# A decoder layer in four token blocks: the last block's side work ordered on four engines, one ring of four PSUM banks, the norm one tile sooner, attention's channels first in the out-projection

## The chip, the cores and the metric

The kernel runs on one core of a Trainium2 chip. The metric is the device time of one execution in microseconds (us). Several executions were timed, and one more was profiled; the rows of the profile and its trace are from that one. PE is TensorE (matrix products), DVE is VectorE, ACT is ScalarE, POOL is GpSimd, SP is SyncE, which here issues the DMAs. A time in a row counts from the start of the span.

## What is computed

One layer (DEPTH is 1) over 2048 tokens of width 1024, all in float32:

```python
h = rmsnorm(x, norm1)
q, k, v, b_gate, c_gate, hc, p = split(h @ w_in)       # 512, 128, 128, 256, 256, 256, 256 columns
attn_out = sliding_window_attention(q, k, v, sinks, rel_bias)   # window 128, 8 heads on 2 K/V heads
conv_out = short_conv_mixer(b_gate, c_gate, hc, conv_w)
pool_out = multiscale_pool_mixer(p, pool_w, pool_scale)
x = x + concatenate([attn_out, conv_out, pool_out]) @ w_out
h2 = rmsnorm(x, norm2)
x = x + square(relu(h2 @ w1)) @ w2
return rmsnorm(x, final_norm)
```

## The kernel before

A product of float32 matrices is made of three: each operand is split into a high part and a low part, and `mm3` (L273) adds high x high, high x low and low x high in one PSUM bank. So every weight tile is loaded by SP, its high part `wh` cast on ACT and its low part `wl` subtracted on POOL (some on DVE), five half tiles ahead of PE. The same split is made of everything that PE multiplies: `xh`/`xl` of the normed input, `pth`/`ptl` of the transposed probabilities, `mxh`/`mxl` of the mixed channels.

**Stage 1** runs over four blocks b of 512 tokens. A block has 14 projection tiles `pj{b}_{i}` of 24 products each, in the order of `IN_ORDER`: K, then queries, V, the pool and conv channels. From the fourth tile on, counted by n, attention runs between the tiles. It has eight units (j, g): 128 tokens j against K/V head g. A unit goes through scores `sc` (PE), `s`, `nm` (DVE), four exponentials (ACT), `rd` and a product (DVE), transposes `pt` (PE), casts `pth` (ACT) and `ptl` (DVE), products `av` with V (PE), copy and sum `ao` (ACT, DVE), and the split into `mxh` (ACT) and `mxl` (DVE or POOL). Each unit writes 128 columns of all four attention channels, rows 4 to 7 of `mxh`; rows 0 and 1 are the pool channels (through `ppm`, in `do_pmix`), rows 2 and 3 the conv channels (`bo`). Then `out_proj` (L715) makes eight tiles `po{b}_{c}` over the eight rows, 24 products each, adds x, stores x1, and sums its squares for the second norm.

PSUM has eight banks: `ps_mm` three for `pj` and `po`, `ps_sc` two for the scores, `ps_tr` two for transposes, norms and `ppm`, and `ps_av` one for `av`.

The next block's first norm is worked off between the out-projection's tiles c: squares at c = 0 and 1 (`norm_square`), the root at 2, its row stored at 3 and broadcast at 4, and the eight channels applied at 5 to 7 (`norm_apply`, rows `hf`, `xh`, `xl`).

In the last block, the second norm of the first 1024 tokens is prepared beside the rest: `first_blocks` (L795 on) loads four x1 tiles `xb` of 128x512 (step 0), scales them on DVE (step 1, four rows of L809) and combines them by four subtractions (step 2, L763), for four channel pairs k at the n that the table `FIRST` gives; the results are stored in `x2s`, whence the MLP reads its operands.

**The MLP** multiplies in two passes of 1024 tokens by a Strassen-like scheme with seven products (`B11`, `T2`, ... in `OPS`); its first products are `bB11`. The second norm of the last block is finished in its first steps, at the keys given to `on` (L1038 to L1040): root, row, broadcast. The second half (`o` tiles) goes over into the final norm: squares on ACT, summed on POOL into `acc3`, root (`final_rstd`), broadcast, scaling of `y` and stores.

The order on each engine is not that of the code: a scheduler places the instructions by priorities and its own idea of their durations, and keeps to buffers and data dependencies. `tc.issue_after(ins)` holds what is issued under it behind `ins`, on the engine of `ins` alone. Before, the last block's side work stood under

```python
with tc.issue_after(latest[0].ins):
```

where `latest[0]` is the last product on PE.

## Time and profile before

| | us |
|---|---|
| median of 3 runs (lowest, highest) | 1937.92 (1937.40, 1938.04) |
| the profiled execution's own time | 1936.93 |
| its span | 1935.2 |
| PE busy in it | 1892.6 |
| block 0's out-projection ends, block 1 begins | 175.9 |
| block 2 begins | 327.5 |
| block 3 begins | 479.1 |
| the MLP's first product | 648.3 |

The page gives busy times and shares of the span; the view of waits names for each engine what it waited for; the windows sum each engine's work between two times; a timeline or a chain of waits has one row for an instruction or a few alike, with its start, its length, its line and, in square brackets, how long the engine was idle before it and what ended that.

### The profile page before, as it was taken

Reading aid. Unit: us, or ns where it says so; the run is one execution under the profiler, and the core shown is the slowest. Engines: PE = TensorE matmul, PEld = TensorE weight load, DVE = VectorE, ACT = ScalarE, POOL = GpSimd, SP = SyncE. Lnnn points to the kernel's source line nnn. Section 1 sums busy time; section 2 is a strip of 40 time slices with the busy share of each in tenths; the row PEclk is TensorE's granted clock in tenths of the full one; section 3 lists DMA queues with packets and bytes.
Section 4 is the critical chain, followed back from the end, with each engine's and each line's share of the span. In section 5 each row is a group of like instructions: output and inputs, shape, how many; then the busy total and the mean of one; then the engine's idle time right before and its main releaser. Section 6 shows DMA issues by size and latency. Waiting matters only on the chain.

```text
span 1935.2 us, 25620 instructions
## 1 busy us (share of the span) xinstructions
PE 1892.6 (98%) x8507; PEld 1527.8 (79%) x8507; DVE 1123.6 (58%) x1423; ACT 895.9 (46%) x1640; POOL 1020.0 (53%) x748
## 2 busy tenths in 40 slices
PE   8999999999899999999999999999999999999997
PEld 5877887887687788888888888888888888888887
DVE  5785686585888577756574444442425264533465
ACT  5664674564367344554575545442323222225332
POOL 5666557565463655654464444434565665526521
PEclk9999999999899999999999999999999999999998
DMA  7327316425935779756685655578777566645344
GB/s 255 102 65 225 108 61 217 126 66 174 300 117 178 233 272 335 255 197 212 216 288 194 196 185 189 186 270 279 235 231 240 191 218 200 221 123 169 96 158 134
DMA packets 194136, 373.34 MB, mean 193 GB/s; under 512 B 22167, under 2 KB 30420, under 8 KB 194004
## 3 DMA queue, kind: packets, MB, share of 16 engines
q1 hardware_dynamic: 193768, 371.62, 59.6%
q8 instruction: 67, 1.10, 0.2%
q14 instruction: 65, 0.53, 0.1%
q10 hardware_dynamic: 236, 0.09, 0.0%
HBM read 248.41 MB, written 116.93 MB: 189 GB/s over the span
## 4 chain that ended last, share of the span: by engine, by line
PE 83%; DVE 7%; DMA 6%; issue 2%; ACT 1%; POOL 1%; SPq 1%; DVEq 0%; POOLq 0%; ACTq 0%
PE o L274 11%; PE o L275 11%; PE o L276 11%; PE bT L275 6%; PE bT L276 6%; PE bT L274 6%; PE bB L275 5%; PE bB L274 5%; PE bB L276 5%; PE pj L275 4%; PE pj L276 4%; PE pj L274 4%; DMA x1s<-xo 1%; PE pt L604 1%; DVE xl L406 1%
## 5 line engine op out<-in xcount | busy, mean ns | idle before, releaser
L253 POOL TENSOR_TENSOR wl<-wr,wh 128x512 fp32r<-128x512 f32 x354 | 499.2, 1417 | 502.4 <-ACT wh L252 462.1
L252 ACT CAST wh<-wr 128x512 fp32r<-128x512 f32 x416 | 254.3, 617 | 362.5 <-PE bT L275 66.9
L763 DVE TENSOR_TENSOR bl<-br,bh 128x1024 fp32r<-128x1024 f32 (+2 forms) x144 | 186.8, 1300 | 324.7 <-ACT bh L1111 323.8
L275 PE MATMUL o<-bl,wh 128*128 128x512 f32 (+1 forms) x960 | 363.4, 381 | 0.0
L276 PE MATMUL o<-bh,wl 128*128 128x512 f32 (+1 forms) x960 | 362.7, 381 | 0.0
L274 PE MATMUL o<-bh,wh 128*128 128x512 f32 (+1 forms) x960 | 351.1, 381 | 0.0
L275 PEld LDWEIGHTS o<-bl,wh 128*128 128x128 f32 x960 | 180.9, 188 | 38.3 <-DVE bl L763 0.2
L276 PEld LDWEIGHTS o<-bh,wl 128*128 128x128 f32 x960 | 180.8, 188 | 38.2
L274 PEld LDWEIGHTS o<-bh,wh 128*128 128x128 f32 x960 | 176.3, 188 | 38.0
L276 PE MATMUL bT<-hhT,wl 128*128 128x512 f32 x512 | 203.7, 398 | 0.0
L275 PE MATMUL bT<-hlT,wh 128*128 128x512 f32 x512 | 203.6, 398 | 0.0
L274 PE MATMUL bT<-hhT,wh 128*128 128x512 f32 x512 | 203.4, 398 | 0.0
L274 PE MATMUL pj<-xh,wh 128*128 128x512 f32 x440 | 176.7, 403 | 10.6 <-ACT wh L252 6.7
L275 PE MATMUL pj<-xl,wh 128*128 128x512 f32 x440 | 177.5, 403 | 6.1 <-DVE xl L406 5.8
L276 PE MATMUL pj<-xh,wl 128*128 128x512 f32 x440 | 176.2, 401 | 0.0
L253 POOL TENSOR_TENSOR wl<-s,wh 128x512 fp32r<-128x512 f32 x64 | 91.2, 1426 | 141.5 <-ACT wh L252 130.9
L252 ACT CAST wh<-s 128x512 fp32r<-128x512 f32 x64 | 39.7, 621 | 250.1 <-PE o L275 249.9
L275 PE MATMUL bB<-hlB,wh 128*128 128x512 f32 x384 | 152.3, 397 | 0.7 <-DVE hlB L967 0.7
L274 PE MATMUL bB<-hhB,wh 128*128 128x512 f32 x384 | 152.5, 397 | 0.0
L1111 ACT CAST bh<-br 128x1024 fp32r<-128x1024 f32 (+2 forms) x144 | 123.2, 857 | 63.3 <-PE o L276 57.6
L276 PE MATMUL bB<-hhB,wl 128*128 128x512 f32 x384 | 152.0, 396 | 0.0
L220 POOL TENSOR_TENSOR s<-wr,wr 128x512 f32<-128x512 f32 x64 | 128.5, 2008 | 14.9 <-DMA wr<-in_w_dram 10.2
(188 smaller groups left out, 3388.0 us busy)
## 6 DMA issues: line engine op xcount, KB each, us to landing
wr<-in_w_dram SPq DMA_DIRECT2D x256, 256.0 KB, 3.8
hop_T<-s SPq DMA_DIRECT2D x128, 256.0 KB, 3.1
wr<-in_win_dram SPq DMA_DIRECT2D x112, 256.0 KB, 4.4
hop_B<-h SPq DMA_DIRECT2D x96, 256.0 KB, 3.3
br<-hop_B SPq DMA_DIRECT2D x48, 512.0 KB, 4.4
br<-hop_T SPq DMA_DIRECT2D x48, 512.0 KB, 4.3
wr<-in_wout_dram SPq DMA_DIRECT2D x64, 256.0 KB, 2.9
wr<-ss_T SPq DMA_DIRECT2D x48, 256.0 KB, 2.8
```

What stands on the lines that cost most here:

```text
L220: gp.tensor_tensor(out=t, in0=a, in1=b, op=op)
L252: act.copy(hi, src)
L253: eng.tensor_tensor(out=lo, in0=src, in1=f32(hi), op=ALU.subtract)
L274: pe.matmul(ps, hi, xh, start=first, stop=False)
L275: pe.matmul(ps, hi, xl, start=False, stop=False)
L276: return pe.matmul(ps, lo, xh, start=False, stop=last)
L406: dve.tensor_tensor(out=xl[:, k], in0=hf, in1=f32(xh[:, k]), op=ALU.subtract)
L604: pe.transpose(ps[:, m * P : (m + 1) * P], s[:, m, kh * P : (kh + 1) * P], ident)
L763: return dve.tensor_tensor(out=out, in0=a, in1=b, op=ALU.subtract)
L1111: mark["act"] = act.copy(hi, src)
```

## The change

- `behind()` takes the place of `issue_after(latest[0].ins)`: it holds the last block's side work behind the latest instruction in the code on each of ACT, DVE, POOL and SP. `FIRST` moves some of its steps one n later.
- `ps_mm` has four banks, which `pj`, `av`, `ppm` and `po` share; `ps_av` is gone.
- `out_proj` multiplies rows 4 to 7 (attention) first, then 0 to 3, and its weights are loaded in that order.
- `do_pool(b, 1)` and `do_pmix(b, 1)` come one tile later.
- The next block's norm: all squares at c = 0, and every step one tile sooner, two channels applied at each of c = 4 to 7.
- The second norm of the last block takes its root, row and broadcast at (0, 1, 2), (0, 2, 4) and (0, 3, 2) in place of (0, 0, 2), (0, 1, 4) and (0, 3, 0).
- At the end, the last four squares are not added on POOL; PE sums them in PSUM by eight more products with a column of ones. The last stores go out from SP and ACT in turn.

```diff
-FIRST = ((0, 1, 2), (0, 3, 4), (3, 5, 6), (5, 7, 8))
+FIRST = ((0, 2, 3), (0, 3, 4), (4, 6, 7), (5, 7, 8))
...
+    sides = {e.engine for e in (act, dve, gp, sp)}
...
         for t in [win[c] for c in IN_ORDER] + [wout[c] for c in range(KC)]:
-            plan += [(plan_load(h), None) for h in halves(t)]
+            hs = halves(t)
+            plan += [(plan_load(h), None) for h in (hs if t.tensor is win.tensor else hs[::-1])]
...
+    @contextmanager
+    def behind():
+
+        with ExitStack() as order:
+            seen = set()
+            for ins in reversed(nc.cur_bb.bb.instructions):
+                if ins.engine in sides and ins.engine not in seen:
+                    seen.add(ins.engine)
+                    order.enter_context(tc.issue_after(ins))
+                    if len(seen) == len(sides):
+                        break
+            yield
...
-    ps_mm, s1 = opened("ps_mm", bufs=3, space=PSUM)
+    ps_mm, s1 = opened("ps_mm", bufs=4, space=PSUM)
...
-    ps_av, s4 = opened("ps_av", bufs=1, space=PSUM)
...
-    def rstd_of(acc, r, offs, psp, tag, name):
+    def rstd_of(accs, r, offs, psp, tag, name):
...
+        accs = accs if isinstance(accs, list) else [accs]
         for j, o in enumerate(offs):
-            pe.matmul(ps[:, j : j + 1], acc[:, o : o + P], ones, start=True, stop=True)
+            for i, acc in enumerate(accs):
+                pe.matmul(ps[:, j : j + 1], acc[:, o : o + P], ones, start=i == 0, stop=i == len(accs) - 1)
...
     def att_av(b, j, g, pts):
-        av = ps_av.tile([P, T], F32, tag="av", name=f"av{b}_{j}_{g}")
+        av = ps_mm.tile([P, T], F32, tag="mm", name=f"av{b}_{j}_{g}")
...
     def do_pmix(b, i):
         oh, ol = ct["p", i]
-        ps = ps_tr.tile([P, T], F32, tag="tr", name=f"ppm{b}_{i}")
+        ps = ps_mm.tile([P, T], F32, tag="mm", name=f"ppm{b}_{i}")
...
-        for k in range(KC):
-            if k % HC == 0:
+        for n in range(KC):
+            k = (n + HC) % KC
+            if n % HC == 0:
                 hi, lo = w_next()
...
-            mm3(ps, hi[:, k % HC], lo[:, k % HC], mxh[:, k], mxl[:, k], k == 0, k == KC - 1)
+            mm3(ps, hi[:, k % HC], lo[:, k % HC], mxh[:, k], mxl[:, k], n == 0, n == KC - 1)
...
             elif n == 7:
+                do_pmix(b, 0)
+            elif n == 8:
                 do_pool(b, 1)
-                do_pmix(b, 0)
-            elif n == 9:
+            elif n == 10:
                 do_pmix(b, 1)
...
-                with tc.issue_after(latest[0].ins):
+                with behind():
...
-                if c < 2:
-                    for k in range(2 + c * 6 // 2, 2 + (c + 1) * 6 // 2):
+                if c == 0:
+                    for k in range(2, KC):
                         norm_square(b + 1, k, dve)
+                elif c == 1:
+                    norm_rstd(b + 1)
                 elif c == 2:
-                    norm_rstd(b + 1)
+                    row_store(nr[b + 1], "n1", (b + 1) * T, T, ps_tr, "tr", f"n1_{b + 1}", tmp(f"row1_{b}"))
                 elif c == 3:
-                    row_store(nr[b + 1], "n1", (b + 1) * T, T, ps_tr, "tr", f"n1_{b + 1}", tmp(f"row1_{b}"))
-                elif c == 4:
                     norm_bcast(b + 1)
                 else:
-                    for k in {5: (0, 1), 6: (2, 3, 4), 7: (5, 6, 7)}[c]:
+                    for k in (2 * (c - 4), 2 * (c - 4) + 1):
                         norm_apply(b + 1, k)
...
-    on((0, 0, 2), norm2_rstd, NB - 1, psb, "b")
-    on((0, 1, 4), lambda: norm2_row(NB - 1, psb, "b", um("row2")))
-    on((0, 3, 0), norm2_bcast, 1)
+    on((0, 1, 2), norm2_rstd, NB - 1, psb, "b")
+    on((0, 2, 4), lambda: norm2_row(NB - 1, psb, "b", um("row2")))
+    on((0, 3, 2), norm2_bcast, 1)
...
-    def final_mul(p, n, f, cs):
+    def final_mul(p, n, f, cs, eng=sp):
...
-        late.append(lambda: sp.dma_start(outT[f * P : (f + 1) * P, a + cs.start : a + cs.stop], t))
+        late.append(lambda: eng.dma_start(outT[f * P : (f + 1) * P, a + cs.start : a + cs.stop], t))
...
+    w = TH // 2
+    acc3[1, 0] = [acc3[1, 0]]
     for j in range(HC):
-        final_square(1, 0, 2 * j + 1, cs, False)
+        if j % 2 == 0:
+            sq = pG.tile([P, TH], F32, tag="sq", name=f"sql_{j}", bufs=2)
+        t = sq[:, j % 2 * w : j % 2 * w + w]
+        act.activation(t, y_of(1, 2 * j + 1, 0, cs), AF.Square)
+        acc3[1, 0].append(t)
...
     for f in range(KC):
-        final_mul(1, 0, f, cs)
+        final_mul(1, 0, f, cs, act if f % 2 else sp)
         flush()
```

The order of instructions on the engines, at the three places that the prediction speaks of. (Lines in the changed kernel are 13 to 16 higher. The last number of a name is a running number.)

PE, block 1, the last two units of attention (`av1_2_1` and `av1_3_1`) and the first products of the out-projection. Before:

```order
L604 MATMUL pt1_2_1_1_2940<-ident_160,s1_2_1_2787 128x128 x4
L276 MATMUL pj1_7_3050<-xh1_1844,wl71_2908 128x512
L615 MATMUL av1_2_1_2961<-pth1_2_1_0_2936,VV_443 128x512
L616 MATMUL av1_2_1_2961<-ptl1_2_1_0_2937,VV_443 128x512
L604 MATMUL pt1_3_1_0_2998<-ident_160,s1_3_1_2880 128x128 x4
L274 MATMUL po1_0_3101<-mxh_446,wh72_2925 128x512
L275 MATMUL po1_0_3101<-mxl_447,wh72_2925 128x512
...
L615 MATMUL av1_3_1_3028<-pth1_3_1_1_3012,VV_443 128x512
L274 MATMUL po1_0_3101<-mxh_446,wh72_2925 128x512
L274 MATMUL po1_1_3152<-mxh_446,wh74_2992 128x512
L616 MATMUL av1_3_1_3028<-ptl1_3_1_1_3013,VV_443 128x512
```

And of the change, first at unit `av1_2_1`, ahead of tile `pj1_11`, then at the last unit, behind tile `pj1_7`:

```order
L617 MATMUL pt1_2_1_0_2921<-ident_160,s1_2_1_2784 128x128 x4
L629 MATMUL av1_1_1_2854<-ptl1_1_1_1_2839,VV_440 128x512
L617 MATMUL pt1_2_1_1_2930<-ident_160,s1_2_1_2784 128x128 x4
L628 MATMUL av1_2_1_2951<-pth1_2_1_0_2926,VV_440 128x512
L289 MATMUL pj1_11_2970<-xh1_1797,wh68_2723 128x512
...
L289 MATMUL ppm1_1_3082<-poh1_1_2966,pwh_435 128x512
L629 MATMUL av1_3_1_3025<-ptl1_3_1_0_3001,VV_440 128x512
L628 MATMUL av1_3_1_3025<-pth1_3_1_1_3009,VV_440 128x512
L629 MATMUL av1_3_1_3025<-ptl1_3_1_1_3010,VV_440 128x512
L290 MATMUL ppm1_1_3082<-pol1_1_2967,pwh_435 128x512
L291 MATMUL ppm1_1_3082<-poh1_1_2966,pwl_436 128x512
L289 MATMUL po1_0_3107<-mxh_443,wh72_2915 128x512
```

A unit's `av` was spread through a projection tile or between products of the out-projection. Now its first product stands ahead of the next tile, and the last unit's products stand directly ahead of the out-projection, whose first product (half tile `wh72`) reads the attention rows in place of the pool rows.

ACT, block 1, the copies and casts at the same place in the change (`ao` and `mxh` of the last unit, `sq2` the squares of the next block's norm, `mxh` of `ppm` and of `bo`):

```order
L636 COPY ao1_3_1_3036<-av1_3_1_3025 64x512
L389 ACTIVATE sq2_2_3088<-xr2_2_2306 128x512
L720 ACTIVATE mxh_443<-ppm1_1_3082,prm_159 128x512
L389 ACTIVATE sq2_3_3091<-xr2_3_2406 128x512
L667 CAST mxh_443<-bo1_1_3078 128x512
L641 CAST mxh_443<-ao1_3_1_3036 64x4x128
```

Before, the row of `ppm` stood ahead of this stretch; the other five are the same.

DVE, the out-projection of block 2, where block 3's norm is applied (`hf`, `xl`; `xo` ends an out-projection tile). Before:

```order
L406 TENSOR_TENSOR xl3_4867<-hf3_0_4868,xh3_4866 128x512
L406 TENSOR_TENSOR xl3_4867<-hf3_1_4872,xh3_4866 128x512
L809 SCALAR_TENSOR_TENSOR xb0_1_5263<-xb0_1_5263,prm_159,rb2_0_acc_5259 128x512
L724 TENSOR_TENSOR xo2_5_4876<-po2_5_4877,xo2_5_4876 128x512
L404 SCALAR_TENSOR_TENSOR hf3_2_4920<-xr3_2_3820,prm_159,rb3_4820 128x512
L404 SCALAR_TENSOR_TENSOR hf3_3_4924<-xr3_3_3920,prm_159,rb3_4820 128x512
L404 SCALAR_TENSOR_TENSOR hf3_4_4928<-xr3_4_4021,prm_159,rb3_4820 128x512
```

The change there, and further on in block 3 ahead of the last unit (`s3_3_1`):

```order
L422 TENSOR_TENSOR xl3_4820<-hf3_0_4821,xh3_4819 128x512
L422 TENSOR_TENSOR xl3_4820<-hf3_1_4825,xh3_4819 128x512
L738 TENSOR_TENSOR xo2_4_4829<-po2_4_4830,xo2_4_4829 128x512
L420 SCALAR_TENSOR_TENSOR hf3_2_4873<-xr3_2_3817,prm_159,rb3_4773 128x512
...
L607 TENSOR_TENSOR s3_2_1_5853<-s3_2_1_5853,rd3_2_1_5858 128x4x256
L823 SCALAR_TENSOR_TENSOR xb2_0_5657<-xb2_0_5657,prm_159,rb2_0_rb_5255 128x512
L823 SCALAR_TENSOR_TENSOR xb2_1_5658<-xb2_1_5658,prm_159,rb2_0_acc_5256 128x512
L823 SCALAR_TENSOR_TENSOR xb2_2_5659<-xb2_2_5659,prm_159,rb2_0_rb_5255 128x512
...
L606 RECIPROCAL rd3_3_1_5956<-den3_3_1_5955 128x4
```

The xb rows, of which three stood among the last rows of `hf` and `xl` and five more behind them, have left the out-projection of block 2: all 32 now stand inside block 3, eight of them ahead of the last unit's `rd`.

More of the change, by code (lines that the diff above doesn't have):

```diff
@@ L1 @@
 import math
-from contextlib import ExitStack
+from contextlib import ExitStack, contextmanager
 import numpy as np
@@ L275, in mm3 @@
         pe.matmul(ps, hi, xl, start=False, stop=False)
-        return pe.matmul(ps, lo, xh, start=False, stop=last)
+        pe.matmul(ps, lo, xh, start=False, stop=last)
     prm = cst.tile([P, NPAR], F32, name="prm")
@@ L482, in tile_trunk @@
     first = {}
-    latest = [None]
     def start_first(tiles):
@@ L510, in proj @@
                     mid()
-                latest[0] = mm3(ps, hi[:, k % HC], lo[:, k % HC], xh[:, k], xl[:, k], k == 0, k == KC - 1)
+                mm3(ps, hi[:, k % HC], lo[:, k % HC], xh[:, k], xl[:, k], k == 0, k == KC - 1)
         return ps
@@ L717, in out_proj @@
         ps = ps_mm.tile([P, T], F32, tag="mm", name=f"po{b}_{c}")
-        for k in range(KC):
-            if k % HC == 0:
+        for n in range(KC):
+            k = (n + HC) % KC
+            if n % HC == 0:
                 hi, lo = w_next()
-            if k == 0:
+            if n == 0:
                 sp.dma_start(xo, xT[c * P : (c + 1) * P, b * T : (b + 1) * T])
-            mm3(ps, hi[:, k % HC], lo[:, k % HC], mxh[:, k], mxl[:, k], k == 0, k == KC - 1)
+            mm3(ps, hi[:, k % HC], lo[:, k % HC], mxh[:, k], mxl[:, k], n == 0, n == KC - 1)
         dve.tensor_tensor(out=xo, in0=ps, in1=xo, op=ALU.add)
@@ L923, in tile_trunk @@
     flush()
-    for st in (sX, sB, s4, s3, s2, s1):
+    for st in (sX, sB, s3, s2, s1):
         st.close()
@@ L1142, in final_rstd @@
         r = cst.tile([P, 6], F32, tag="nr3", name=f"r3_{p}_{n}_{cs.start}", bufs=2)[:, : len(offs)]
-        rstd_of(acc3[p, n][:, cs], r, offs, psb, "b", f"n3_{p}_{n}_{cs.start}")
+        a = acc3[p, n]
+        rstd_of([a[0][:, cs]] + a[1:] if isinstance(a, list) else a[:, cs], r, offs, psb, "b", f"n3_{p}_{n}_{cs.start}")
         r3[p, n, cs.start] = r
```

## The prediction

> **What bounds the kernel now.** The page first (busy us, share of the span, instructions):
>
> ```profile
> PE 1892.6 (98%) x8507; PEld 1527.8 (79%) x8507; DVE 1123.6 (58%) x1423; ACT 895.9 (46%) x1640; POOL 1020.0 (53%) x748
> ```
>
> PE fills 98% of the span and no other engine comes near, so what counts is where PE stands still and where its clock is halved. The view of what PE waits for lists the standstills (us in total, times, longest), and the last row is the same view of 478 to 494 us alone:
>
> ```profile
> PE pj L275 <- DVE xl L406: 5.8, 7, 2.9
> PE sc L577 <- DMA q<-ql: 3.6, 5, 2.2
> PE pst_n L314 <- POOL acc L942: 3.5, 1, 3.5
> PE av L615 <- DVE ao L624: 3.2, 4, 1.9
> PE pj L274 <- ACT xh L405: 1.7, 1, 1.7
> PE pst_n L314 <- POOL acc L732: 1.2, 1, 1.2
> ...
> PE pj L275 <- DVE xl L406: 3.8, 3, 2.9
> ```
>
> Apart from the first load and the tail, these are nearly all the standstills there are. Next, sums over stretches of time: start:end and length, busy time of PE, PEld, DVE, ACT and POOL with instruction counts, granted clock of PE, DMA share, GB/s.
>
> ```profile
> 175.00:285.00 110.00, 108.42 (x535) 88.78 (x534) 76.45 (x106) 68.35 (x158) 68.54 (x63) 1.00 0.39 114
> 480.00:600.00 120.00, 108.61 (x506) 86.57 (x505) 104.04 (x134) 65.23 (x151) 65.64 (x51) 0.94 0.58 187
> 486.40:493.20 6.80, 3.89 (x9) 2.65 (x9) 6.80 (x7) 1.96 (x4) 3.85 (x3) 0.50 0.86 262
> 517.10:520.50 3.40, 3.12 (x9) 2.31 (x9) 2.21 (x4) 0.00 (x0) 0.00 (x0) 0.50 1.05 380
> 595.60:602.40 6.80, 6.35 (x19) 4.95 (x20) 5.87 (x10) 4.40 (x8) 1.28 (x1) 0.50 0.04 15
> 660.50:663.90 3.40, 3.40 (x9) 2.62 (x9) 1.21 (x2) 1.79 (x4) 0.00 (x0) 0.50 0.94 305
> ```
>
> Two things are seen. Block 1 (175 to 285) leaves DVE 33 us of slack; block 3 (480 to 600) has DVE busy for 104 of 120 us. And a standstill of PE costs twice: after the 2.9 us at 486, the 2.2 us at 516, the 1.9 us at 593 to 596 and the 1.2 us at 658, PE ran 3.4 or 6.8 us at half clock, half of which is lost.
>
> The Trainium skill ("TensorE: Matmul & The Clock Gate", section "What's actually happening") says that the array goes to half clock only after at least one idle window of about 3.4 us. The rows above disagree: standstills of 1.2 to 2.9 us were enough. By that rule of the Trainium skill my sum below would be 3.4 us less; it goes by the rows.
>
> **The change part by part.** *One ring of four banks, attention's channels first* (blocks 1 and 2). The rows of PE's order show two new things. First, `av` now takes a bank of the projections' ring, so its first product has to stand ahead of the next projection tile, directly behind the transposes that it needs: `av1_2_1` has 0.6 us of PE work (one `av` product and four transposes) between `pt1_2_1_0` and itself. In that time ACT must cast the transpose:
>
> ```profile
> 281.17 0.58 ACT L607 CAST pth<-pt 128x512 fp32r<-128x512 f32 x1
> 283.67 0.58 ACT L623 COPY ao<-av 64x512 f32<-64x512 f32 x1 [0.69 <-PE av L616]
> 284.28 1.16 ACT L373 ACTIVATE sq<-xr 128x512 f32<-128x512 f32 x2
> 285.33 0.60 ACT L654 CAST mxh<-bo 128x512 fp32r<-128x512 f32 x1
> 285.96 0.62 ACT L628 CAST mxh<-ao 64x512 fp32r<-64x512 f32 x1
> ```
>
> The cast is 0.58 us, behind up to one other ACT row of 0.6 us. So a unit waits for 0 to 0.8 us; walking the units of block 1 along ACT's order I get six waits of 0.15 to 0.8 us, **2.8 us** in all (bounds 0, if ACT always runs ahead, and 5).
>
> Second, the start of the out-projection. Each unit writes 128 columns of all four attention channels, so the first product of channel 4 needs the last unit. Before, channels 0 to 3 of three tiles stood there and covered it:
>
> ```profile
> 281.93 0.50 PE L615 MATMUL av<-pth,VV 128*128 128x512 f32 x1 [0.31 <-DVE ao L624]
> 283.19 0.40 PE L616 MATMUL av<-ptl,VV 128*128 128x512 f32 x1
> 288.34 0.40 PE L274 MATMUL po<-mxh,wh 128*128 128x512 f32 x1
> 289.04 0.40 PE L274 MATMUL po<-mxh,wh 128*128 128x512 f32 x1
> ```
>
> The last `av` product starts at 283.19 and the last `mxh` cast ends at 285.96 + 0.62 = 286.58: 3.4 us of chain (0.2 us of product, copy, two squares, cast of `bo`, cast of `ao`). Nobody saw it, since the attention half of the weights begins at 289.04 only. In the new order nothing but two `ppm` products (2 x 0.23 us) stands between the last `av` and the first `po`, and ACT's queue has the same rows plus the `ppm` cast (0.69 us, in place of one idle moment). PE waits 3.4 + 0.4 - 0.5, or **3.3 us** (bounds 2.0, if only copy 0.58, add 0.7, cast 0.62 and their hand-overs count, and 4.0). After a standstill of that length the rows above say one stretch of 3.4 us at half clock: **1.7 us** (bounds 0 and 3.4).
>
> What goes in these blocks: the 0.3 us of `av` on `ao` and the waits for `xl` at the block's start, since the next block's norm is worked off a tile sooner. Of their 5.8 us, 3.8 lie at the last seam, so 2.0 us in four waits are shared by two seams: 1.0 each. Per block 2.8 + 3.3 + 1.7 - 0.3 - 1.0 = +6.5, for two blocks **+13.0** (bounds +2 and +22).
>
> *Block 0.* DVE is what it waits for: busy 38.16 us of the 41 before its out-projection.
>
> ```profile
> 95.00:136.00 41.00, 37.63 (x168) 28.36 (x166) 38.16 (x52) 26.73 (x60) 24.63 (x23) 0.92 0.17 55
> ```
>
> The change takes nothing off DVE there; the waits move from inside the units to the start of the out-projection. I take **+1** (bounds -4, PE's own lost 41 - 37.6 us with the clock, and +5.5, the same stall and clock as block 1).
>
> *The last block's xb work ordered on four engines.* This gives the seam 2 to 3 back to `xl`: the 3.8 us at 479 to 490, the late `xh` of 1.7 us, and the half clock after it (6.8 / 2 = 3.4). In the same block go the 2.2 us wait for `q<-ql` with its clock (1.7), and by the fourth bank the 1.9 us with its clock (3.4). That would be 18 us. But the xb rows are not gone: in the new order all 32 stand between the third unit's scores and the last `mxl`. DVE's rows from 480 to 610 (busy, mean ns | idle):
>
> ```profile
> L763 DVE TENSOR_TENSOR xb<-xb,xb 128x512 f32<-128x512 f32 x16 | 13.1, 839 | 0.1
> L809 DVE SCALAR_TENSOR_TENSOR xb<-xb,prm,rb_rb 128x512 f32<-128x512 f32 x8 | 8.4, 1075 | 1.6 <-DMA xb<-x1s 1.6
> L406 DVE TENSOR_TENSOR xl<-hf,xh 128x512 fp32r<-128x512 f32 x6 | 8.1, 1403 | 0.0
> L809 DVE SCALAR_TENSOR_TENSOR xb<-xb,prm,rb_acc 128x512 f32<-128x512 f32 x7 | 7.4, 1051 | 2.2 <-DMA xb<-x1s 2.2
> L404 DVE SCALAR_TENSOR_TENSOR hf<-xr,prm,rb 128x512 f32<-128x512 f32 x3 | 3.1, 1076 | 0.0
> ```
>
> ```profile
> 479.08 0.40 PE L274 MATMUL pj<-xh,wh 128*128 128x512 f32 x1
> 599.69 0.78 PE L274 MATMUL po<-mxh,wh 128*128 128x512 f32 x1
> 648.33 0.40 PE L274 MATMUL bB<-hhB,wh 128*128 128x512 f32 x1
> 608.04 0.69 DVE L629 TENSOR_TENSOR mxl<-ao,mxh 64x512 fp32r<-64x512 f32 x1
> ```
>
> Block 3 starts at 479.08 and the MLP at 648.33: 169.25 us. The last `mxl` comes 129.0 us in, 8.4 us behind the first product of the out-projection, hidden again by channels 0 to 3. After the change the first scores stand behind four projection tiles (96 x 0.233 = 22.4 us, by the three products from 288.34 to 289.04) and some 4 us of small products and hand-over: DVE's part can begin 27 us in. It is 104.04 us less `xl` 8.1 and `hf` 3.1, which stand ahead of it, or 93; some early `ql` rows off and the last 9 us of the block on leave about 91. Of the 16 us in which DVE stood idle from 480 to 600, most fall to waits inside the units that the xb rows can now fill; walking the order I leave 4. So the last unit is ready 27 + 91 + 4 = 122 us in, its `mxh` at 121. Then come 192 products, 44.8 us, 1.7 us of half clock and 1 us of leftovers: 168.5 against 169.25. I take **0** (bounds -5, no idle DVE, and +7, 11 us of the 16 idle). The 18 us are given back as waits for DVE inside the units and at the out-projection, which has lost its cover.
>
> *The MLP's start.* The square sums of the last norm stand one row of products later, when POOL has long added: the 1.2 us, a following 0.3 and half of the 3.4 us at 660.5 go, **-3.2** (bounds -4, if the next wait goes with it, and -1.2).
>
> *The tail.*
>
> ```profile
> 1920.04 0.75 ACT L1136 ACTIVATE sq<-y 128x256 f32<-128x256 f32 x2 [3.67 <-DVE y L942]
> 1920.53 3.12 POOL L942 TENSOR_TENSOR acc<-sq,acc 128x256 f32<-128x256 f32 x4 [19.09 <-ACT sq L1136]
> 1928.78 3.77 SPq L1156 DMA_DIRECT2D out_dram<-y  x8
> 1929.14 2.35 DVE y L1152 x6
> ```
>
> POOL's four additions end at 1923.65. Without them four squares, two in 0.75 us, end 1.5 us behind 1920.04 or, with their waits for `y`, by 1921.8: 1.85 us sooner. The eight more products of 128x1 take some of it; no row has their price ahead of others, and at 0.08 us each, a third of the 0.23 of a full one, they cost 0.65: -1.2. SP issues a store each 3.77 / 8 = 0.47 us behind a DVE row each 2.35 / 6 = 0.39; two queues save the difference, 8 x 0.08 = -0.6. Together **-1.8** (bounds -3 and 0).
>
> Sum: 13.0 + 1 + 0 - 3.2 - 1.8 = **+9.0** on the profiled execution's own 1936.93 us, 1945.9. The median of the runs is 1937.92, 1.0 higher: 1946.9.
>
> **The rivals.** *PE sets block 3 after all.* If the xb rows run at their shortest (0.74 and 0.67 us against means of 1.06 and 0.84) DVE's part is 8 us shorter:
>
> ```profile
> L763 DVE TENSOR_TENSOR xb<-xb,xb x16: 670/679/1769, 499.1 to 540.6; 128x512 f32<-128x512 f32 x16
> L809 DVE SCALAR_TENSOR_TENSOR xb<-xb,prm,rb_rb x8: 734/752/1791, 492.7 to 524.7; 128x512 f32<-128x512 f32 x8
> ```
>
> PE's own work in block 3 is 169.25 less 18, or 151; with 2.8 + 3.3 + 1.7 that is 159, a gain of 10: sum -1, 1937. The long ones beside POOL speak against it.
>
> *The other side: ACT and DVE run a tile ahead.* With four banks PE takes up attention sooner; if ACT's casts are always there, no unit waits, and only the data's own chain of 2.0 us with 1.7 of clock is left: blocks 1 and 2 +2.4 each, block 3 at 151 + 3.7 = 154.7, -14.5, the rest -4: sum -13.7, 1924. It decides if the last `mxl` of block 3 comes before 110 us. For it: 33 us of DVE slack in block 1. Against it: the ACT rows between `av` and `mxh`, which stand there whatever DVE does.
>
> *DVE is later still in block 3*: each unit's wait holds up the next one's scores, since PE, ACT and DVE stand in each other's order; 10 us more, 1957.
>
> *The clock stays full after a standstill of 3.3 us*: 2 x 1.7 less, 1943.5. That is what the Trainium skill's rule would give. The four half-clock rows speak against it.
>
> That the xb work doesn't move is excluded by DVE's order, where the seam has none of its rows any more.
>
> **How the numbers follow.** Forecast 0.45, PE sets block 3 0.17, a tile ahead 0.20, later still 0.12, full clock 0.06. Some 0.2% (3.9 us) is what a measurement of this kernel tells from no change, so faster is under 1934.0 and slower over 1941.8. Faster: 0.20 and a little of the second case, 0.22. Same: 0.15 of the second and 0.05 of the forecast's low end, 0.20. Slower: the rest, 0.58. The range goes from 1927 (leaving out half of the tile-ahead case) to 1957 (half of the later case).
>
> **What would show it.** In the new profile: a wait of PE at each `po`, first row, on ACT's `mxh` of some 3 us in blocks 1 and 2, with a half-clock stretch behind it; small waits of `av` on `pth`; no wait for `xl` over 1 us at the last seam; block 3 near 169 us with DVE busy over nine tenths from 27 us on; no `pst_n` wait on L732; the tail's `pst_n` at about 1922. It is wrong if the out-projection starts without a wait, or if block 3 comes out under 160 us.

## The result, and the profile after

The changed kernel takes 1966.41 us in the median of 4 runs (1964.81 to 1967.01) against 1937.66 us (1935.4 to 1938.04, 4 runs) of the kernel before in the same sittings: ratio 1.015, 95% interval 1.0132 to 1.0167. It is slower, as forecast, but by 28.8 us where 9 were forecast, and above the range. Beside the runs of e1 to e4, one execution of the kernel before and one of e4 took over three times as long (6580 and 6490 us); they are left out of every figure.

The profiled execution took 1965.88 us, 28.95 more than that of before (1936.93). Cut at the first projection product of each block and at the MLP's first product, its trace gives (us):

| | block 0 | block 1 | block 2 | block 3 | MLP to the end |
|---|---|---|---|---|---|
| before | 175.9 | 151.6 | 151.6 | 169.2 | 1286.8 |
| after | 191.7 | 159.2 | 159.8 | 170.8 | 1282.7 |
| difference | +15.8 | +7.5 | +8.3 | +1.5 | -4.2 |
| forecast | +1 | +6.5 | +6.5 | 0 | -5.0 |

Four of the five terms came near, the last of them in part by luck, as the experiments show. Block 0 did not, and its 14.8 us too much are three quarters of the error.

The view of PE's waits, after (us in total, times, longest):

```profile
PE po L289 <- ACT mxh L641: 15.0, 4, 6.3
PE av L628 <- ACT pth L620: 9.9, 14, 2.1
PE sc L590 <- DMA q<-ql: 5.9, 2, 4.7
PE pt L617 <- DVE s L607: 2.5, 1, 2.5
PE sc L590 <- DVE s L594: 2.1, 2, 1.3
...
PE pj L290 <- DVE xl L415: 0.4, 2, 0.3
PE pst_n L330 <- ACT sql L1251: 0.3, 1, 0.3
```

The old waits are gone or small: `xl` from 5.8 to 0.4 us, and the waits of `pst_n` on POOL (1.2 and 3.5 us) are none, with 0.3 us on ACT in their place. Two new ones lead, the out-projection on the last unit's cast (four times, once a block) and `av` on the casts of the transposes. The third, scores waiting for a DMA, stands in block 0. The windows (start:end and length, busy PE, PEld, DVE, ACT, POOL, clock, DMA share, GB/s), first of before, then of after, show what the forecast had missed:

```profile
53.00:71.00 18.00, 17.46 (x87) 14.41 (x88) 12.13 (x16) 9.47 (x26) 12.19 (x13) 1.00 0.38 110
```

```profile
53.00:71.00 18.00, 9.14 (x36) 7.31 (x35) 11.50 (x19) 8.03 (x24) 2.43 (x4) 0.65 0.57 151
512.00:632.00 120.00, 109.03 (x511) 87.67 (x509) 93.78 (x130) 64.49 (x149) 61.24 (x47) 0.96 0.56 178
537.70:632.00 94.30, 83.33 (x392) 66.63 (x390) 85.99 (x110) 55.04 (x133) 48.15 (x37) 0.95 0.52 176
461.20:468.00 6.80, 6.50 (x15) 4.64 (x16) 4.55 (x6) 2.75 (x6) 1.33 (x1) 0.50 0.01 2
```

At block 0's first attention units PE made 36 products in 18 us instead of 87, at 0.65 of its clock. Block 3 (510.7 to 681.5) has DVE busy 93.8 of the 120 us from 512 on, 10 less than before; from 27 us into the block DVE is busy 86.0 of 94.3 us, the nine tenths that the prediction named as a sign. The last row is the half clock behind the out-projection's wait in block 2.

Block 1's out-projection on PE and ACT in the timeline of after (start, length, and in brackets idle time before and what ended it):

```profile
298.13 0.40 PE L628 MATMUL av<-pth,VV 128*128 128x512 f32 x1
298.37 0.39 PE L629 MATMUL av<-ptl,VV 128*128 128x512 f32 x1
298.60 0.39 PE L290 MATMUL ppm<-pol,pwh 128*128 128x512 f32 x1
298.83 0.39 PE L291 MATMUL ppm<-poh,pwl 128*128 128x512 f32 x1
302.32 0.97 PE L289 MATMUL po<-mxh,wh 128*128 128x512 f32 x3 [3.10 <-ACT mxh L641]
```

```profile
298.80 0.58 ACT L636 COPY ao<-av 64x512 f32<-64x512 f32 x1 [0.54 <-PE av L629]
299.40 0.63 ACT L389 ACTIVATE sq<-xr 128x512 f32<-128x512 f32 x1
299.94 0.67 ACT L720 ACTIVATE mxh<-ppm,prm 128x512 fp32r<-128x512 f32 x1
300.51 0.62 ACT L389 ACTIVATE sq<-xr 128x512 f32<-128x512 f32 x1
301.03 0.61 ACT L667 CAST mxh<-bo 128x512 fp32r<-128x512 f32 x1
301.66 0.61 ACT L641 CAST mxh<-ao 64x512 fp32r<-64x512 f32 x1
```

This is the chain that the prediction had read from the trace of before: on ACT a copy, two squares, the rows of `ppm` and `bo`, and the cast that PE waits for, back to back, and 3.10 us of wait where 3.3 were forecast.

### The profile page after: what moved, and what is told of

Read it like the earlier page. It is cut to its first block, busy times and chain, and to the rows that moved or that the text cites. A ratio compares the mean times of both kernels' runs of the same rounds, so it can differ in the third digit from the quotient of the medians.

```text
span 1964.1 us, 25655 instructions
## 1 busy us (share of the span) xinstructions
PE 1904.0 (97%) x8523; PEld 1537.2 (78%) x8523; DVE 1131.5 (58%) x1423; ACT 900.8 (46%) x1640; POOL 1025.1 (52%) x744
## 4 chain that ended last, share of the span: by engine, by line
PE 88%; DVE 5%; ACT 3%; DMA 2%; issue 1%; POOL 0%; SPq 0%; DVEq 0%; ACTq 0%; POOLq 0%
PE o L289 11%; PE o L290 11%; PE o L291 11%; PE bT L291 6%; PE bT L290 6%; PE bT L289 6%; PE bB L290 4%; PE bB L289 4%; PE bB L291 4%; PE pj L289 4%; PE pj L290 4%; PE pj L291 4%; PE po L290 3%; PE po L289 3%; PE po L291 3%
## 5 line engine op out<-in xcount | busy, mean ns | idle before, releaser
L255 POOL TENSOR_TENSOR wl<-wr,wh 128x512 fp32r<-128x512 f32 x354 | 506.8, 1436 | 574.5 <-ACT wh L254 526.0
L289 PE MATMUL bB<-hhB,wh 128*128 128x512 f32 x384 | 152.4, 397 | 0.0
```

What stands on the lines that cost most here:

```text
L255: eng.tensor_tensor(out=lo, in0=src, in1=f32(hi), op=ALU.subtract)
L289: pe.matmul(ps, hi, xh, start=first, stop=False)
```

## The experiments

Each run's blocks, from its own profiled execution (us; the last column is the run's difference to before in those executions' spans). e5 to e8, e11 to e13, e16 and e17 are single runs; of the others the profiled execution is one of several, and not always a middle one: that of e3 was the longest of five (1951.7 us, median 1947.5), that of e2 the shortest of four.

Pairs of runs with the same order of instructions say how far such numbers carry. Before, e10 and e14 have the same order on every engine up to the MLP, and differ by up to 4.7 us in block 0 and 1.9 in blocks 1 and 2. e5 and e17 have it in block 3, but for one row moved on each of PE, DVE and ACT, and differ by 6.5 us there. The change, e13 and e16 have the same order on PE in the whole MLP, and differ by up to 4.8 us there. Smaller differences of single executions say nothing by themselves.

| run | block 0 | 1 | 2 | 3 | MLP on | all |
|---|---|---|---|---|---|---|
| before | 175.9 | 151.6 | 151.6 | 169.2 | 1286.8 | |
| after | 191.7 | 159.2 | 159.8 | 170.8 | 1282.7 | +28.9 |
| e1, ring undone | 181.4 | 159.0 | 158.5 | 176.2 | 1285.4 | +25.3 |
| e2, attention first undone | 187.5 | 155.9 | 155.4 | 167.9 | 1282.8 | +14.2 |
| e3, both undone | 182.5 | 153.1 | 156.4 | 170.0 | 1288.0 | +14.7 |
| e4, xb order alone | 175.4 | 151.5 | 152.3 | 175.3 | 1286.8 | +6.1 |
| e5, av one tile later | 188.4 | 156.9 | 156.9 | 174.4 | 1283.8 | +25.1 |
| e6, ring alone | 186.3 | 155.0 | 155.8 | 181.5 | 1284.6 | +28.0 |
| e7, attention first alone | 181.7 | 159.3 | 158.2 | 172.8 | 1284.9 | +21.6 |
| e8, pool later alone | 181.5 | 153.1 | 154.8 | 167.9 | 1287.0 | +9.0 |
| e9, norm, norm2, tail | 174.6 | 154.5 | 150.4 | 168.1 | 1290.0 | +2.4 |
| e10, norm2, tail | 174.9 | 153.5 | 152.2 | 168.6 | 1288.3 | +2.4 |
| e11, all but the xb order | 191.7 | 158.4 | 159.2 | 173.0 | 1282.6 | +29.7 |
| e12, squares behind the last unit | 191.2 | 157.3 | 157.2 | 173.1 | 1286.6 | +30.1 |
| e13, block 0's av out of the ring | 192.6 | 159.5 | 158.4 | 172.9 | 1287.4 | +35.5 |
| e14, tail alone | 179.7 | 152.4 | 153.4 | 168.8 | 1284.5 | +3.5 |
| e15, norm, tail | 177.4 | 154.4 | 150.7 | 170.1 | 1287.6 | +5.0 |
| e16, pj0_2 behind the broadcast | 186.5 | 158.4 | 159.2 | 170.3 | 1285.7 | +24.9 |
| e17, e16 and e5 | 185.4 | 155.3 | 156.1 | 180.9 | 1283.1 | +25.7 |

### e1 to e4: parts undone, and the xb order alone

e1 takes the ring out of the change:

```diff
-    ps_mm, s1 = opened("ps_mm", bufs=4, space=PSUM)
+    ps_mm, s1 = opened("ps_mm", bufs=3, space=PSUM)
...
+    ps_av, s4 = opened("ps_av", bufs=1, space=PSUM)
...
-        av = ps_mm.tile([P, T], F32, tag="mm", name=f"av{b}_{j}_{g}")
+        av = ps_av.tile([P, T], F32, tag="av", name=f"av{b}_{j}_{g}")
...
-        ps = ps_mm.tile([P, T], F32, tag="mm", name=f"ppm{b}_{i}")
+        ps = ps_tr.tile([P, T], F32, tag="tr", name=f"ppm{b}_{i}")
```

> The change with the ring alone undone (three banks for the projections and the out-projection, one for av, the pool mix back in the transposes' banks). Theory R (the shared ring: a projection tile can't take its bank before av of the unit ahead has taken one, so PE stands at block 0's first scores with no tile to work on): block 0 ends 12 to 14 us sooner (near 178 us instead of 191.7), the waits of av on pth (9.9 us) fall under 2 us, the wait at the out-projection (3 us a block) stays; in all near 1948 us. Rival D (block 0 is late since DVE is, by the pool work issued one tile later and the earlier norm): block 0 ends within 3 us of 191.7, in all 1958 to 1963 us.

Measured: 1961.9 us, ratio to before 1.0115 (1.0099 to 1.0131). Block 0 is 10.3 us shorter, less than theory R's 12 to 14 but far from D's 3, so the ring does cost there; the waits of `av` on `pth` vanish from block 1. The total misses R's 1948 us: block 3 is 5.4 and the MLP 2.8 us longer, which no theory had, and blocks 1 and 2 gain nothing, since with a bank of its own the last unit's `av` waits for `ao` instead (block 1's waits):

```profile
PE po L289 <- ACT mxh L645: 2.6, 1, 2.6
PE av L632 <- DVE ao L641: 2.2, 1, 2.2
```

e2 puts the out-projection back in its old order (`for k in range(KC)`, the weights as before).

> The change with the order of the out-projection alone undone (pool and conv channels first, weights loaded in that order); the ring stays. Theory O (the out-projection has lost its cover): the waits of po on mxh (15.0 us in the change) fall under 2 us, blocks 1 and 2 take 153 to 155 us instead of 159.2 and 159.8; block 0's first scores still wait 8 to 9 us and half its 13 us loss or more stays, block 0 near 188 us; in all 1945 to 1950 us. Rival (the wait at the out-projection only moves): PE waits as long a few products later, for channels 4 to 7, and the time falls by under 4 us, 1962 to 1966.

Measured: 1953.75 us, ratio 1.0076 (1.0058 to 1.0094). In block 1 the wait of `po` is 0.2 us, not 3.1, and does not come again at channels 4 to 7:

```profile
PE av L630 <- ACT pth L622: 2.5, 4, 1.4
PE po L288 <- DVE ao L639: 0.2, 1, 0.2
```

Blocks 1 and 2 are 3.3 and 4.4 us shorter, block 0 4.2. The total missed its upper end by 4 us; in the part that theory O is about it stands.

e3 has both undone.

> The change without the ring and without attention's channels first: what is left is the xb work behind four engines, the pool work one tile later, the norm one tile sooner, the second norm's later keys and the tail. If the two parts taken out carry the whole loss: blocks 0 to 2 as before the change or 1 us shorter each, block 3 by 5 to 10 us shorter than 169 us, MLP and tail 4 us shorter: near 1924 us (1918 to 1930). Rival (block 3's DVE with all xb rows inside it is the bound, or the earlier norm takes DVE time from the last units): 1934 to 1942 us.

Measured: 1947.48 us, ratio 1.004 (1.0025 to 1.0055), slower than both cases expected: what is left of the change is no gain, and block 0 is still 6.6 us longer than before. e8 asks whether the later pool mix does that.

e4 puts the xb order alone into the kernel before (`behind()` and `FIRST`).

> The kernel before with only the xb work ordered behind the four engines and the FIRST table of the change. Theory S (the xb rows at the last seam cost PE what the seam lost): the 3.8 us wait for xl and the 1.7 us for xh at 479 to 490 and the half clock behind them (3.4) go, block 3 is 5 to 9 us shorter, in all 1929 to 1933 us. Rival (block 3 is bound by DVE, so the xb rows cost the same inside it): block 3 within 2 us of 169 us, 1936 to 1940 us.

Measured: 1945.92 us, ratio 1.0027 (1.0012 to 1.0043); slower, against both. The seam's `xl` waits do fall to 1.4 us, yet block 3 is 6.1 us longer. Its waits there:

```profile
PE av L630 <- DVE ptl L622: 3.5, 4, 1.5
PE po L288 <- DVE xo L738: 2.9, 1, 2.9
PE pt L618 <- DVE mxl L722: 2.8, 1, 2.8
PE pj L288 <- ACT ct L650: 2.3, 1, 2.3
PE pj L288 <- DVE bo L667: 1.7, 1, 1.7
```

Most wait for DVE rows, which here stand among xb rows: from 580 to 612 us DVE is busy 31.3 of 32 us. The xb work does not cost the same inside block 3 as at the seam, it costs more.

### e5 to e8: the ring's order, and each part alone

e5 issues each unit's `av` in the middle of the next tile, so that this tile takes its bank first:

```diff
+            av = []
             def mid(n=n):
+                if 3 <= n < 11:
+                    av.append(att_av(*st2.pop(n - 1)))
                 if 2 <= n < 10:
                     st2[n] = att_trans(*st1.pop(n - 2))
...
-            if 2 <= n < 10:
-                av = att_av(*st2.pop(n))
```

> The whole change, the ring of four kept, but each unit's av is issued in the middle of the next projection tile, so that this tile takes its bank first. Theory R (what counts in block 0 is that av stands ahead of the next tile in the ring): the tiles pj0_12 and pj0_13 stand ahead of av0_0_0 and av0_1_0, PE's waits between 53 and 71 us fall from 8.8 to under 4 us, block 0 takes 180 to 184 us instead of 191.7, and av no longer waits for pth (9.9 us to under 3). The wait of po on mxh stays at 3 us a block or grows; in all 1950 to 1957 us. Rival (the ring costs by its number of banks, whatever its order): block 0 188 us or more, in all over 1960 us.

Measured: one run, 1962.12 us. The waits from 53 to 71 us fall from 8.8 to 5.6 us, where theory R had under 4, and block 0 is only 3.3 us shorter, at 188.4 us: block and total are the rival's.

e6 has the ring alone, e7 attention's channels first alone, e8 the later second pool mix alone, each in the kernel before.

> The kernel before with the ring of four as the only edit. Theory R: block 0 takes 184 to 188 us against 175.9, blocks 1 and 2 are 2.5 to 4 us longer than 151.6 (waits of av on pth), in all 1950 to 1956 us. Rival (the ring alone is harmless, it needs the later pool work or the earlier norm beside it): block 0 under 179 us, in all under 1943 us.

> The kernel before with attention's channels first in the out-projection as the only edit. Theory O (lost cover, 3.3 us of chain and 1.7 of half clock a block): blocks 1 and 2 take 156 to 159 us against 151.6, block 3 3 to 8 us more than 169.2, block 0 2 to 6 us more than 175.9; in all 1952 to 1962 us. Rival (only the ring's order exposes the chain): blocks 1 and 2 under 153.5, in all under 1943 us.

> The kernel before with only do_pool(b, 1) and do_pmix(b, 1) one tile later. In the run without ring and attention's channels first, block 0 was 6.6 and block 1 1.4 us longer than before the change. Theory P (the second pool mix comes too late): block 0 180 to 183 us against 175.9, blocks 1 and 2 1 to 2 us more, in all 1943 to 1949 us. Rival N (the earlier norm takes DVE and ACT from the last units): within 2 us of the kernel before in every block.

Measured (one run each, 1965.02, 1958.58 and 1946.02 us). The ring alone costs 10.4 us in block 0 and 3.4 and 4.3 in blocks 1 and 2. Its total is 9 us over what was expected, all in block 3, where two waits lead:

```profile
PE bB L274 <- DVE xo L723: 6.8, 1, 6.8
PE sc L576 <- DVE s L580: 5.8, 2, 4.3
PE pj L275 <- DVE xl L405: 3.4, 2, 2.9
```

Attention first alone costs 7.6 and 6.7 us in blocks 1 and 2, 5.8 in block 0, and 3.5 in block 3; theory O is right on every block, within 0.3 us. The later pool mix alone costs 5.6 us in block 0, as theory P has it. The two hide each other there: with both and no ring (e1) block 0 is 181.4, no longer than with either alone.

### e9, e10, e14, e15: what is left as a gain

> The kernel before with three parts of the change: the norm one tile sooner, the second norm's later keys, and the tail. By the first prediction's terms for them: blocks 1 and 2 0.5 to 1 us shorter each (waits for xl), block 3 0 to 3 us shorter, MLP and tail 3 to 5 us shorter (1282 to 1284 us against 1286.8): 4 to 9 us faster than before in the same job. Rival (the earlier norm takes DVE and ACT time from the last units): block 0 2 us or more longer, in all within 3 us of before.

> The kernel before with the second norm's later keys and the tail only. Blocks as before (within 1 us), MLP and tail 3 to 5 us shorter: 3 to 5 us faster. Rival (the waits at the MLP's start move to the next operand that stands there): under 2 us.

> The kernel before with the tail only (the last four squares summed on PE, stores from two queues). From the last products' start to the end 12.8 us instead of 15.2, all blocks within 1 us of before: 2 to 2.5 us faster, ratio 0.9987 to 0.9990. Rival (the gain is lost at the stores' landing): under 1 us.

> The kernel before with the norm one tile sooner and the tail, without the second norm's later keys, which in the run with all three made the MLP 4 us longer (1277.1 us from its first product to the last tile's, against 1271.6). If those keys did that: MLP back at 1271 to 1273 us, block 0 near 174.7, blocks 1 and 2 together 303 to 305, in all 4 to 6 us faster than before, ratio 0.997 to 0.998. Rival (the earlier norm itself moves the MLP's first operands): MLP 1275 us or more, no faster than before.

Measured, 11 or 12 runs each: e9 1.0011 (1.0001 to 1.0022), e10 0.9996 (0.9983 to 1.0009), e14 0.9993 (0.9982 to 1.0004), e15 0.9991 (0.998 to 1.0001). e9 and e15 were expected 4 to 9 and 4 to 6 us faster than before, e10 3 to 5, e14 2 to 2.5; none shows it, though the interval of e14 still holds its number. The tail itself does what it should: in the traces of e9, e10 and e14 the end comes 12.83 us behind the last product's start, in that of e15 13.12, before 15.24. The other two parts do not show. In e10, with the new keys, no wait of `pst_n` on POOL is left at the MLP's start, but other operands are waited for (waits of 640 to 760 us):

```profile
PE bB L275 <- DVE hlB L969: 2.0, 2, 1.3
PE bT L274 <- ACT hhT L968: 1.0, 1, 1.0
PE bT L275 <- DVE hlT L969: 1.0, 2, 0.7
```

That the keys do it is not shown: e14, without them, waits 0.3 us for `pst_n` and the same 2.0 us for `hlB`, and e15, also without, 3.2 us for `pst_n`. From the MLP's first product to the last, before takes 1271.6 us, e14 1271.65, e10 1275.5, e9 1277.1, e15 without the keys 1274.5, and e6 and e7, which have none of these three parts, 1269.4 and 1269.6. No version of the parts is shown to beat the kernel before.

### e11 and e12: the xb order within the change, and ACT's queue

> The change with the xb work left as it was before (hoisted over the last seam). The ring alone took 181.5 us in block 3, the xb order alone 175.3, both with the rest 170.75. Theory C (the ring holds PE at the last seam's first scores, and the xb rows there make it longer, so with the ring the xb order is worth more than it costs): block 3 178 to 184 us, blocks 0 to 2 as in the change, in all 1970 to 1977 us. Rival (the xb order costs its 6 us here too): block 3 163 to 168 us, in all 1957 to 1961 us.

Measured: one run, 1966.69 us, as the whole change; block 3 takes 173.0 us. Both cases missed. The xb order, worth 6.1 us the wrong way alone, is worth 2.2 the right way here, within the spread. The 181.5 us of the ring alone in block 3 hold a wait of 6.8 us at the MLP's first product that this run doesn't have; e17 has one of 4.5 us there and e5, with nearly the same order, none.

e12 orders the next norm's squares behind the last unit's cast on ACT:

```diff
-        act.copy(hi, o)
+        last_mx[0] = act.copy(hi, o)
...
+                    with tc.issue_after(last_mx[0].ins):
+                        for k in range(2, KC):
+                            norm_square(b + 1, k, dve)
```

> The change, with the next norm's six squares ordered behind the last unit's mxh cast on ACT. If the 3.1 us wait at the out-projection of blocks 1 and 2 is a queue on ACT (two squares of 0.6 us between the copy and the cast), it falls to 2.0 to 2.5 us and the blocks are 0.6 to 1.5 us shorter. Rival (the chain through DVE or the half clock sets it, and ACT's squares lie beside it): 2.9 us or more, blocks within 0.4 us of 159.2 and 159.8.

Measured: one run. The wait in block 1 falls to 2.1 us, blocks 1 and 2 are 1.9 and 2.7 us shorter (the total is lost again in block 3 and at the MLP, by less than the spread of single runs there). Of the 3.1 us, 1.0 is ACT's queue and 2.1 the data's own chain.

```profile
PE po L289 <- ACT mxh L644: 2.1, 1, 2.1
```

### e13, e16, e17: why the ring costs in block 0

e13 takes `av` of block 0 alone out of the ring:

```diff
+        pool, tag = (ps_mm, "mm") if b else (ps_tr, "tr")
-        av = ps_mm.tile([P, T], F32, tag="mm", name=f"av{b}_{j}_{g}")
+        av = pool.tile([P, T], F32, tag=tag, name=f"av{b}_{j}_{g}")
```

> The change, with av of block 0 alone taking a bank of the transposes' pool in place of the projections' ring; all else, and all other blocks, as in the change. Theory R (block 0 is late because av0_0_0 stands ahead of pj0_12 in the ring, so that PE comes to the first scores with no tile left): the waits between 53 and 71 us fall from 8.8 to under 3 us, no half clock there, block 0 takes 179 to 184 us instead of 191.7; blocks 1 and 2 stay at 159 to 160; in all 1953 to 1959 us. Rival (block 0's end is set by DVE and the late pool mix, and the first stall only moves): block 0 188 us or more.

Measured: one run, 1972.5 us. The waits from 53 to 71 us are 1.3 us, without half clock, and block 0 is still 192.6 us. Theory R falls in its simple form: the stall that looked so large is gone and the block is as long as before the edit. Block 0's waits in this run:

```profile
PE pt L620 <- DVE ao L641: 3.3, 2, 1.7
PE sc L593 <- DVE s L597: 2.9, 1, 2.9
PE pt L620 <- DVE s L610: 2.7, 1, 2.7
PE po L289 <- ACT mxh L645: 2.4, 1, 2.4
```

The first of them is of the edit's own making (transposes waiting for the bank that `av` holds), the others are the units' own chain: scores, softmax, transposes.

What the kernels with four banks up to here have in common is another row, the first softmax row on DVE. Before, after, and in e13:

```profile
55.37 0.69 DVE L581 SCALAR_TENSOR_TENSOR s<-sc,bias 128x512 f32<-128x512 f32 x1 [2.05 <-PE sc L578]
```

```profile
62.38 0.69 DVE L594 SCALAR_TENSOR_TENSOR s<-sc,bias 128x512 f32<-128x512 f32 x1 [4.06 <-PE sc L591]
```

```profile
61.41 0.69 DVE L597 SCALAR_TENSOR_TENSOR s<-sc,bias 128x512 f32<-128x512 f32 x1 [0.23 <-PE sc L594]
```

It is the first of eight, one for each unit, and comes 7.0 us later than before. The lateness is not simply kept: the third unit's row comes at 69.7 us against 69.1 before, the fourth at 81.0 against 75.2, the eighth at 116.3 against 108.6. Whether the start sets the rest is what e16 tests. Why the chain starts later stands on PE, in the products that broadcast block 0's norm, without which no tile can be evacuated. Before, after:

```profile
39.33 0.83 PE L356 MATMUL pbc_n<-ident,r 128*128 128x128 f32 x6
```

```profile
36.20 0.39 PE L289 MATMUL pj<-xh,wh 128*128 128x512 f32 x1
...
45.21 1.05 PE L372 MATMUL pbc_n<-ident,r 128*128 128x128 f32 x8
```

The tile `pj0_2` is the fourth to ask for a bank of `ps_mm`. With three banks it had to wait for an evacuation, and so for the broadcast. With a fourth bank PE takes it at 36.20, its 24 products ahead of the broadcast, which comes 5.9 us later. e16 orders that tile behind the broadcast:

```diff
+                if b == 0 and n == 1:
+                    order.enter_context(tc.issue_after(pbc))
                 ps = proj(b, i, mid)
```

> The change, with the products of block 0's tile pj0_2 ordered behind the four products that broadcast the first norm. In all kernels with three banks for the projections the first softmax row s0_0_0 came at 55 to 56 us; in all with four, at 61 to 62, av's place in the ring or not: the fourth bank lets PE take pj0_2 (24 products, 5.6 us) ahead of that broadcast, on which every evacuation of the first tiles waits. Theory L (block 0 is set by the chain of its eight units, which starts 6 us late): s0_0_0 at 55 to 57 us, block 0 takes 183 to 187 us instead of 191.7, blocks 1 and 2 as in the change; in all 1957 to 1961 us. Rival (av's place in the ring sets it): s0_0_0 sooner, but block 0 still 189 us or more.

Measured: one run, 1961.87 us. The broadcast, the first softmax row, and block 0 at 186.5 us, as theory L has it:

```profile
39.97 1.05 PE L372 MATMUL pbc_n<-ident,r 128*128 128x128 f32 x8
```

```profile
56.83 0.69 DVE L597 SCALAR_TENSOR_TENSOR s<-sc,bias 128x512 f32<-128x512 f32 x1 [1.99 <-PE sc L594]
```

Against the change all eight softmax rows come 5.4 to 6.4 us sooner, and the block is 5.2 us shorter: in the order of the ring the start does carry through to the end. Against the kernel before, the rows from the fourth on are back within 1.7 us (the eighth at 109.9 us), and yet the block is 10.6 us longer. What is left of the loss comes behind the last unit's softmax. There the traces of e1, without the ring, and of e16 differ so, first e1, then e16:

```profile
132.11 0.69 DVE L641 TENSOR_TENSOR ao<-av,ao 64x512 f32<-64x512 f32 x1 [1.29 <-ACT ao L640]
132.84 0.61 ACT L645 CAST mxh<-ao 64x512 fp32r<-64x512 f32 x1 [0.76 <-DVE ao L641]
```

```profile
132.53 0.68 DVE L534 TENSOR_TENSOR z<-pj,rb 128x512 f32<-128x512 f32 x1
134.49 0.69 DVE L640 TENSOR_TENSOR ao<-av,ao 64x512 f32<-64x512 f32 x1
136.87 0.61 ACT L644 CAST mxh<-ao 64x512 fp32r<-64x512 f32 x1
```

The last product of the last projection tile starts at 117.0 us in e1 and at 129.8 in e16, between the last unit's `av` products. So in e16 the row that evacuates this tile (`z`) and one of the conv channels stand on DVE ahead of the last unit's sum `ao`, and the cast that the out-projection waits for comes 4.0 us later than in e1. No edit tests this reading.

e17 has e5's edit with it.

> The change with both edits to the order: pj0_2 behind the norm's broadcast, and each unit's av behind the next tile's start. Alone, the first took 5.2 us off block 0 and the second 3.3, of the 10.3 us that undoing the ring takes off. If the late start and av's place are two separate parts of the ring's cost: block 0 takes 181 to 184 us, near the 181.4 without the ring. Rival (the two edits mend the same thing): 186 us or more.

Measured: one run, 1962.66 us; block 0 185.4 us, between the two. The late start is about half of the ring's 10.3 us. For the other half there are only the rows above, and the runs do not settle it, with 4.7 us of spread between executions.

## Why the prediction was right or wrong, point by point

**The out-projection without cover: right.** Forecast 3.3 us a block and 1.7 of half clock, measured 3.10 and 3.09 us in blocks 1 and 2 with 3.4 and 6.8 us at half clock behind them, so 1.7 and up to 3.4 us lost. e2 removes the wait by the order alone, e7 makes it by the order alone.

**The units' waits: right.** Forecast 2.8 us a block in six waits, measured 2.5 in block 1 and in block 2 (four waits of `av` on `pth` each), and the ring alone lengthens blocks 1 and 2 by 3.4 and 4.3 us. Undoing it within the change gains 0.2 and 1.3 us there (e1), within the spread.

**Block 0: the step that failed.** "DVE is what it waits for ... The change takes nothing off DVE there; the waits move" was the step, priced at +1 us where the block became 15.8 us longer. DVE was busy 38 of the 41 us from 95 to 136, but that it set the block's end did not follow; nor are they the time before the out-projection, whose first product starts at 117.6 us and which covered the last units' chain. The runs showed three costs in its place. The ring costs some 10 us (10.4 alone in e6, 10.3 undone in e1): the fourth bank lets PE take `pj0_2` ahead of the norm's broadcast, the chain of units starts 7.0 us later, and putting the tile back gains 5.2 us (e16, one run, little over the spread); the other 5 us stay open. The lost cover of the out-projection costs 5.8 us alone (e7), the later second pool mix 5.6 alone (e8), and both together, with the rest of the change but the ring, 5.5 (e1), the one hiding the other. The later pool mix has no term in the sum at all, which put it at nothing without a reason. The order of PE was read at attention's end, in block 1, and block 0 was priced from those 41 us alone; its start, where the moved tile stands, was not looked at.

**Block 3: right, 0 against +1.5.** The gains at the seam came (`xl` 5.8 to 0.4 us in all, none of it at that seam) and were given back, as forecast, inside the units and at the out-projection, which waited 6.3 us. The sum put the last unit's `mxh` 121 us in and 47.5 us behind it; its cast starts 123.0 us in, and from the first product of the out-projection to the MLP it is 47.1 us. That DVE binds the block with the xb rows inside fits e4, which is slower by that alone. How the total splits on the parts was not as the sum has it: the xb order costs 6.1 us alone and nothing clear of the spread within the change. The same block in e12, e13 and e16 takes 170.3 to 173.1 us, 1.1 to 3.9 more than before.

**MLP and tail: -5.0 forecast, -4.2 measured; the tail right, the rest luck.** The tail's -1.8 became -2.4 (12.8 us in place of 15.2; in some of the runs with the same tail 13.0 to 13.3). The MLP's first products gained 1.8 us in place of 3.2 in this one execution. In e12, e13 and e16, with the same order on PE there, the way from the MLP's first product to its last is 1.3 to 3.0 us longer than before, since other operands are late next, and in e6 and e7 it is 2 us shorter without the new keys. So no run shows the -3.2 us of the keys; and its "following 0.3" stands in no row of before, whose next standstill behind the 1.24 us is one of 0.73 at 670 us.

Of the rivals, "later still" came nearest in size (+19 for the +29) but in the wrong block. The full clock rival fell: after 3.1 us, and in e12 after 2.07, PE ran at least 3.4 us at half speed. The Trainium skill's rule ("TensorE: Matmul & The Clock Gate", "What's actually happening") of one whole idle window of some 3.4 us is not what these traces show. That rival also left out block 3's 1.7 us, so its price was 5.1 us and not 3.4. One row behind it was misread: the half clock at 486.4 us of before starts together with the standstill of 2.9 us, and follows one of 1.7 us.

## What to carry to other kernels

A further buffer lets the scheduler put work of PE further ahead, and what it is put ahead of may be the short product that a whole chain waits for: look where the first piece of the critical chain moves to, at the start of the program too, and not only at the waits that the buffer is to remove. Work that needs the last result of a stage shouldn't stand first in the next stage; the old order of the out-projection hid 3 us of chain a block at no cost. When an engine is 90% busy in a stretch, ask whether it is the bound or only follows a chain. When a large stall is done away with and the block stays as long (e13), it was not the bound. And price every line of the change, also the one that only moves a call: the pool mix one tile later cost 5.6 us in block 0.

## What the runs showed of the hardware

Kernels with the same order on every engine up to the tail (before and e14) differed by 3.8 us in block 0 in two executions, with the first softmax row at 55.4 and 57.5 us. The small DMAs that move `ql` into `q` took 0.9 us longer from issue to landing in e14; their line in the view of the tile `q`, from 40 to 60 us, of before and then of e14:

```profile
DMA to landing us min/median/max: 6.0/6.4/6.9
```

```profile
DMA to landing us min/median/max: 6.9/7.3/7.6
```

The chain behind them was later still: the eighth softmax row came at 108.6 and 113.3 us. That the DMAs began it is read from these rows and not tested. Standstills of PE near 2 us (e12, 2.07 in blocks 1 and 2) were followed by a stretch at half clock of 3.4 us.
